# A streaming SSD and gMLP encoder step: GpSimd's weight subtractions become a negated copy on ScalarE and an adding transfer

## The chip, the core and the metric

The kernel runs on one core of one Trainium2 chip. The metric is the device time of one execution in microseconds. Three runs of the kernel before took 1111.30, 1112.45 and 1113.49 us; the median is 1112.45 us. The profile is one execution of its own, with its own time.

Engines are named as in the profile: PE is TensorE (PEld its weight loads), DVE is VectorE, ACT is ScalarE, POOL is GpSimd, SP is SyncE, which only issues transfers here.

## The reference

640 tokens (512 of a prompt, 8 streams of 16 more) go through two layers of width 1024, both with RMSNorm ahead and a residual add behind.

- Layer A is a Mamba-2 mixer: one projection of 1024 to z (2048), x (2048), B (1024), C (1024) and dt (32); a causal convolution of width 4 with SiLU over x, B and C, whose last three input columns are an output too; a chunked state scan of 32 heads in 8 groups; a gate with z and a group norm; a projection back to 1024.
- Layer B is a gMLP: a projection to u, v and z, a LayerNorm of v, a position mix in each of 8 groups, a gate, a projection back.

All of it is float32 with a tight tolerance. The core of layer A, cut:

```
proj = h @ w_in                      # z | x | B | C | dt
xp = concat([conv_prev, xbc]); out = b + sum(w[k] * xp[:, k:k + seq_len])
h_new = h * exp(last) + einsum(B, w_in, x); y = y_in + y_st
return (group_rms_norm(y * silu(z))) @ w_out, xp[:, seq_len:], h_new
```

## The kernel before

**Numbers.** PE multiplies in a reduced float32 format, so each operand is split in two: H is the value rounded to that format, L the rest. A product is three matrix multiplications, H times H, H times L and L times H. For the tokens the tiles are xH and xL, for the weights wh and wl.

**A weight tile** is 128 rows by 1024 columns, 512 KB. `wsplit` (L93 to L104) makes one ready: SP fetches it into `raw` (L95, two buffers), ACT rounds it into `wh` (L99), and then `wl = raw - wh` is made by an engine that the caller names (L100): DVE or POOL. `wh` and `wl` have four buffers each, and a buffer comes free when PE has used the tile.

**The stream of layer A** holds 64 such tiles in the order of their use: for each of the 8 groups x0, x1, B, C, z0, then in the groups 1 to 6 two tiles "o" of the output projection of the group before, then z1; in the first two groups a few stand elsewhere. `Stream.next` hands out a tile and first asks for those that follow, up to `ahead` = 2 (L110 to L135). The set `on_pool` (L316) says whose subtraction POOL makes: the tiles 3 to 6, all z0 and all twelve "o" but the last four tiles of the stream. That is 23 of 63; DVE makes the other 40 (the first tile has its own code).

**A group of layer A.** PE projects x0, x1, B and C tile by tile. Behind each projection `conv_tile` (L406 to L429) does the convolution: DVE moves the result out of PSUM into `xp` with the norm's factor (L411 to L413); POOL clears three columns and copies the cached ones in (L409, L410) and copies the last ones out for the output `nconv` (L415, L416); ACT does the first tap (L418), DVE the other three, each an instruction with two inputs in SBUF (L421); ACT and DVE do the SiLU (L427, L428) into `xc`. PE transposes `xc` to tokens (L468, tile `tp`) for the scan. POOL also makes `xw` (L480), decays old states (L586) and masks some decays `E` (L630). Meanwhile DVE does a chain of five-column steps for the norm (L77 to L86), and ACT the decays `E` of the four heads (L514, L515), which SP reads from `laD` (L512).

**The order.** PE's order is that of the program. In layer A, that of ACT, DVE, POOL and SP is set by a list scheduler when the program is built; each engine then runs its own list strictly in order and waits on semaphores. Layer B (from about 630 us) has its order written out and is touched by none of the changed lines.

Of the kernel before, what the change touches and what calls it, by code (L numbers as in the profile page):

```python
# [8 lines left out]
F32 = mybir.dt.float32  # L9
F32R = mybir.dt.float32r  # L10
I32 = mybir.dt.int32
AF = mybir.ActivationFunctionType
ALU = mybir.AluOpType
# [27 lines left out]
def hybrid_step(ctx: ExitStack, tc: tile.TileContext, xin, xT0, cst, wdt, cache, wA, wAo, h0in, wB, wBv, wBo,  # L41
                lnwb, spc, bsp, nwb, y_out, nconv_out, sspP_out, sspS_out, v_out):
    nc = tc.nc
    V, S, G, T = nc.vector, nc.scalar, nc.gpsimd, nc.tensor
# [17 lines left out]
    def C(n):  # L62
        a, b = _C[n]
        return csb[0][:, a:b] if b <= NCST1 else csb[1][:, a - NCST1:b - NCST1]
# [28 lines left out]
    def wsplit(eng, pool, src, scale=None):  # L93
        raw = (pool or wpool).tile([P, 1024], F32, name="raw", tag="raw", bufs=2)
        nc.sync.dma_start(out=raw, in_=src)  # L95
        H = wpool.tile([P, 1024], F32R, name="wh", tag="wh", bufs=4)
        L = wpool.tile([P, 1024], F32R, name="wl", tag="wl", bufs=4)
        if scale is None:
            S.copy(out=H, in_=raw)  # L99
            eng.tensor_tensor(out=L, in0=raw, in1=H.bitcast(F32), op=ALU.subtract)  # L100
        else:
            S.activation(H, raw, AF.Identity, scale=scale)
            V.scalar_tensor_tensor(L, raw, scale, H.bitcast(F32), ALU.mult, ALU.subtract)
        return H, L  # L104

    class Stream:
# [3 lines left out]
        def fill(self, ahead):  # L110
            while len(self.got) < min(len(self.srcs), self.n + ahead):
                i = len(self.got)
                self.got.append(wsplit(G if i in on_pool else V, self.pools.get(i), *self.srcs[i]))
# [144 lines left out]
    def in_proj(W, xT, pool=None, tag="in", at=(1, 3, 5, 7, 9, 11, 13)):  # L258
        outs = []
        for h, (a, b) in enumerate(HALVES):  # L260
            o = (pool or ps_in).tile([P, 512], F32, name="pin", tag=tag)[:, :b - a]
            outs.append(o)
            for k in range(KD):
                in_proj_step(W, xT, o, h, k)
                if 8 * h + k in at:
                    pump()
        return outs
# [33 lines left out]
    def wo(g):  # L301
        return [(wAo[f],) for f in (2 * g, 2 * g + 1)]

    units, names = [], []
# [8 lines left out]
        names += [p[0] for p in part]  # L313
        units += [p[1:] for p in part]
    units += wo(GROUPS - 2) + wo(GROUPS - 1)
    on_pool = {3, 4, 5, 6} | {i for i, n in enumerate(names) if n in ("z0","o")}  # L316
    stream = Stream(units, 2)


    with ExitStack() as ca:  # L320
# [35 lines left out]
        for d in (15, 13, 11, 9, 7, 5, 3):  # L356
# [17 lines left out]
                        in1=C("blk").rearrange("p (b o) -> p b o", o=1).broadcast_to([P, 8, HEADS]), op=ALU.mult)  # L374
# [31 lines left out]
        def conv_tile(o0, o1, ft, j, cch, nconv):  # L406
            xp = w1.tile([P, 667], F32, name="xp", tag="xp")
            xps = xp[:, 515:667].rearrange("p (b j) -> p b j", j=19)
            G.memset(xp[:, 0:3], 0.0)  # L409
            G.tensor_copy(out=xps[:, :, 0:3], in_=cch[:, j])  # L410
            V.tensor_tensor(out=xp[:, 3:387], in0=o0, in1=rb[:, 0:384], op=ALU.mult)  # L411
            V.tensor_tensor(out=xp[:, 387:515], in0=o1[:, 0:128], in1=rb[:, 384:512], op=ALU.mult)
            V.tensor_tensor(out=xps[:, :, 3:19], in0=o1[:, 128:256].rearrange("p (b j) -> p b j", j=16),  # L413
                            in1=rb[:, 512:640].rearrange("p (b j) -> p b j", j=16), op=ALU.mult)
            G.tensor_copy(out=nconv[:, j, 0, :], in_=xp[:, 512:515])  # L415
            G.tensor_copy(out=nconv[:, j, 1:9, :], in_=xps[:, :, 16:19])  # L416
            acc = w1.tile([P, 667], F32, name="acc", tag="acc")
            S.activation(acc[:, 0:664], xp[:, 0:664], AF.Identity, scale=cw[:, 4 * ft:4 * ft + 1],  # L418
                         bias=cw[:, 128 + ft:129 + ft])
            for k in range(1, 4):  # L420
                V.scalar_tensor_tensor(acc[:, 0:664], xp[:, k:k + 664], cw[:, 4 * ft + k:4 * ft + k + 1], acc[:, 0:664],  # L421
                                       ALU.mult, ALU.add)
            xc = w1.tile([P, NT], F32, name="xc", tag="xc", bufs=5)
            accs = acc[:, 515:667].rearrange("p (b j) -> p b j", j=19)[:, :, 0:16]
            xcs = xc[:, 512:].rearrange("p (b j) -> p b j", j=16)
            for o, a in ((xc[:, :512], acc[:, :512]), (xcs, accs)):
                S.activation(o, a, AF.Tanh)  # L427
                V.scalar_tensor_tensor(o, o, 1.0, a, ALU.add, ALU.mult)  # L428
            return xc  # L429

        cio = conv_io(0)
        pB = in_proj(stream.next(), xT, ps_y, "y")
        xcs = [conv_tile(*o, ft, j, *cio) for j, (o, ft) in enumerate(((px0, 0), (px1, 1), (pB, 16)))]
        side += [cum_sums] + [lambda h=h: by_heads(*h) for h in HALVES]
        pC = in_proj(stream.next(), xT, at=(2, 9, 11))
# [4 lines left out]
        wk = ca.enter_context(tc.tile_pool(name="wk", bufs=2))  # L440

        xcs.append(conv_tile(*pC, 24, 3, *cio))
        pend = {}
        for g in range(GROUPS):
            last = g == GROUPS - 1
            hsl = slice(4 * g, 4 * g + 4)
            if g > 1:
                cio = conv_io(g)
                xcs = [conv_tile(*in_proj(stream.next(), xT), 2 * g, 0, *cio)]
                side.append(pss_)  # L450
                xcs.append(conv_tile(*in_proj(stream.next(), xT, at=(9,)), 2 * g + 1, 1, *cio))
                pump(9)
# [69 lines left out]
            if g:  # L522
                queue(0, *(() if g == 1 else (0,)))
                o = in_proj(stream.next(), xT, ps_m, "m", at=(3, 7, 11, 14))
                xcs.append(conv_tile(*o, 16 + g, 2, *cio))
                queue(1, *(() if g == 1 else (1,)))
                o = in_proj(stream.next(), xT, at=(3, 7, 11, 14))
# [686 lines left out]
```

## Time and profile before

| what | value |
|---|---|
| median of three runs | 1112.45 us (1111.30 to 1113.49) |
| the profiled execution's own time | 1110.38 us |
| its span from the first to the last instruction | 1108.6 us |
| busy share of PE, DVE, ACT, POOL | 94%, 81%, 40%, 18% |
| subtractions of wl on POOL | 23, 55.9 us in all |
| subtractions of wl on DVE in layer A | 40, 50.2 us in all |
| reads from HBM | 106.93 MB |

Busy shares are means over two very different layers. PE is nearly always busy; where it is not, the table of waits names what it waited for. A duration of an engine includes any time that the instruction is held up after its start, so the spread of durations of one kind of instruction is worth as much attention as the mean.

### The profile page before, as it was taken

The page shows a single profiled execution, that of the slowest core. Times are in us where ns is not written, and L with a number is a line of the kernel's source. Part 1 is how long each engine was busy: PE and PEld are TensorE (multiplying, and loading weights), DVE is VectorE, ACT ScalarE, POOL GpSimd, SP SyncE. Part 2 cuts the span into 40 slices and gives each one's busy share as a digit, 9 for nine tenths or more (in the row PEclk, how much of TensorE's full clock was granted, in tenths as well). Part 3 has the DMA queues.
Part 4 walks back from the last instruction along what each step waited for, and adds up shares of the span by engine and source line. Part 5 has one row for each costly group of instructions (what it writes and reads, how often), then busy time and mean ns, then how long its engine had stood idle before and what let it go on. Part 6 is the DMA issues. An engine that isn't in the chain of part 4 may idle for free.

```text
span 1108.6 us, 16897 instructions
## 1 busy us (share of the span) xinstructions
PE 1040.2 (94%) x6387; PEld 936.6 (84%) x6387; DVE 899.4 (81%) x1573; ACT 441.1 (40%) x801; POOL 200.7 (18%) x303
## 2 busy tenths in 40 slices
PE   8998899898998998999999899996899999999996
PEld 7897889798898797888997678886888988988985
DVE  6969897888878878888789866656889889889876
ACT  6363515326254162262552343245333433433343
POOL 2434322404214224042132000000000000000000
PEclk9899999999999999999999999999999999999998
DMA  6463535243362352432622512211423412412322
GB/s 243 146 181 96 170 94 183 85 156 123 91 211 79 89 194 85 156 120 92 211 82 72 171 52 77 69 41 53 124 64 92 124 61 92 122 62 93 89 67 95
DMA packets 56928, 124.88 MB, mean 113 GB/s; under 512 B 9072, under 2 KB 27760, under 8 KB 56848
## 3 DMA queue, kind: packets, MB, share of 16 engines
q1 hardware_dynamic: 56848, 123.82, 35.1%
q8 instruction: 50, 0.82, 0.3%
q14 instruction: 30, 0.25, 0.1%
HBM read 106.93 MB, written 16.86 MB: 112 GB/s over the span
## 4 chain that ended last, share of the span: by engine, by line
PE 53%; DVE 31%; ACT 8%; DMA 4%; issue 3%; SPq 0%; POOL 0%; ACTq 0%; DVEq 0%
PE pop L69 14%; PE pin L69 11%; DVE acc L421 7%; PE pv L69 7%; PE pqb L69 5%; PE pqa L69 4%; PE pqc L69 4%; DMA E<-laD 3%; DVE wf L748 2%; PE st L69 2%; DVE E L630 2%; PE yB L69 1%; DVE xc L428 1%; ACT E L514 1%; DVE rt L85 1%
## 5 line engine op out<-in xcount | busy, mean ns | idle before, releaser
L69 PE MATMUL pin<-xH,wh 128*128 128x384 f32 (+1 forms) x768 | 251.0, 327 | 9.4 <-DVE xp L411 8.6
L69 PE MATMUL pin<-xH,wl 128*128 128x384 f32 (+1 forms) x768 | 240.7, 313 | 0.5 <-DVE wl L100 0.5
L69 PE MATMUL pin<-xL,wh 128*128 128x384 f32 (+1 forms) x768 | 240.5, 313 | 0.0
L69 PEld LDWEIGHTS pin<-xH,wh 128*128 128x128 f32 x768 | 148.4, 193 | 17.7 <-ACT xc L427 9.6
L69 PEld LDWEIGHTS pin<-xL,wh 128*128 128x128 f32 x768 | 148.5, 193 | 0.4 <-issue 0.3
L69 PEld LDWEIGHTS pin<-xH,wl 128*128 128x128 f32 x768 | 147.9, 193 | 0.8 <-DVE wl L100 0.8
L421 DVE SCALAR_TENSOR_TENSOR acc<-xp,cw,acc 128x664 f32<-128x664 f32 x96 | 114.3, 1191 | 17.9 <-ACT acc L418 16.6
L69 PE MATMUL pop<-wf,yHL 128*128 128x512 f32 x480 | 115.3, 397 | 1.1 <-DVE h L964 0.4
L69 PEld LDWEIGHTS pop<-wf,yHL 128*128 128x128 f32 x480 | 89.2, 188 | 25.2 <-DVE h L964 3.1
L748 DVE TENSOR_TENSOR wf<-raw,wf 128x512 fp32r<-128x512 f32 x128 | 86.5, 685 | 29.3 <-ACT wf L747 28.3
L69 PE MATMUL pop<-wh,yHL 128*128 128x512 f32 x320 | 103.4, 404 | 5.8 <-DVE hs L565 5.4
L99 ACT CAST wh<-raw 128x1024 fp32r<-128x1024 f32 x63 | 65.6, 1041 | 103.4 <-PE pin L69 64.7
L747 ACT CAST wf<-raw 128x512 fp32r<-128x512 f32 x128 | 76.4, 617 | 53.9 <-PE pop L69 27.2
L69 PEld LDWEIGHTS pop<-wh,yHL 128*128 128x128 f32 x320 | 57.8, 188 | 21.5 <-DVE hs L565 7.9
L69 PE MATMUL pqa<-xH,wf 128*128 128x320 f32 x256 | 64.3, 320 | 7.3 <-ACT c L1011 7.3
L685 DVE SCALAR_TENSOR_TENSOR h<-pop,rr,h 128x512 f32<-128x512 f32 x80 | 59.0, 743 | 12.7 <-PE pop L69 12.4
L69 PE MATMUL pv<-wh,xL 128*128 128x512 f32 x160 | 62.9, 393 | 2.4 <-DVE xL L231 2.4
L69 PE MATMUL pv<-wh,xH 128*128 128x512 f32 x160 | 63.5, 397 | 0.9 <-DVE xL L231 0.8
L69 PE MATMUL pqb<-tf,wf 128*128 128x320 f32 x384 | 63.0, 313 | 0.9 <-DVE zz L1026 0.9
L69 PE MATMUL pv<-wl,xH 128*128 128x512 f32 x160 | 63.0, 394 | 0.0
L69 PE MATMUL pop<-wl,yHL 128*128 128x512 f32 x160 | 62.6, 391 | 0.0
L514 ACT ACTIVATE E<-E,la 128x128 f32<-128x128 f32 x160 | 51.6, 389 | 17.1 <-DMA E<-laD 12.9
(221 smaller groups left out, 2018.5 us busy)
## 6 DMA issues: line engine op xcount, KB each, us to landing
raw<-wA SPq DMA_DIRECT2D x47, 512.0 KB, 3.8
raw<-wB SPq DMA_DIRECT2D x32, 512.0 KB, 4.0
E<-laD SPq DMA_DIRECT2D x32, 320.0 KB, 6.8
h<-h0in SPq DMA_DIRECT2D x16, 512.0 KB, 4.8
raw<-wAo SPq DMA_DIRECT2D x16, 512.0 KB, 4.1
out_sspS<-h SPq DMA_DIRECT2D x16, 512.0 KB, 3.9
raw<-wBv SPq DMA_DIRECT2D x16, 512.0 KB, 4.2
raw<-wBo SPq DMA_DIRECT2D x16, 512.0 KB, 3.8
```

The lines of the kernel that those rows point to most:

```text
L69: T.matmul(out, lhsT=lhsT, rhs=rhs, start=start, stop=stop, **kw)
L85: V.scalar_tensor_tensor(t, t, -0.5, x, ALU.mult, ALU.mult)
L99: S.copy(out=H, in_=raw)
L421: V.scalar_tensor_tensor(acc[:, 0:664], xp[:, k:k + 664], cw[:, 4 * ft + k:4 * ft + k + 1], acc[:, 0:664], ALU.mult, ALU.add)
L428: V.scalar_tensor_tensor(o, o, 1.0, a, ALU.add, ALU.mult)
L514: S.activation(E_[:, t, :], E_[:, t, :], AF.Relu, bias=la[:, t, h:h + 1], scale=-1.0)
L630: (G if i and (last or e) else V).tensor_tensor(out=Es[2 * i + e], in0=Es[2 * i + e], in1=CBm, op=ALU.mult)
L685: V.scalar_tensor_tensor(h1[:, t, dsl], ps, rg[:, t:t + 1], h1[:, t, dsl], ALU.mult, ALU.add)
L747: S.copy(out=t[:, 0], in_=src)
L748: V.tensor_tensor(out=t[:, 1], in0=src, in1=t[:, 0].bitcast(F32), op=ALU.subtract)
```

## The change

Four edits, all in layer A.

1. For the tiles in `on_pool`, POOL no longer subtracts. ACT writes `-wh` into `wl`, and POOL issues a transfer that reads the weight tile from HBM a second time and adds it to what stands in `wl`.
2. The set `on_pool` loses the tiles 3, 5 and 6, whose subtraction goes to DVE: 20 tiles are left on POOL, 43 are on DVE.
3. The memset of three columns in `conv_tile` goes from POOL to DVE, and its three small copies from POOL to ACT.
4. `ahead` is 3 in place of 2. The buffers stay as many as they were.

```diff
@@ wsplit
             S.copy(out=H, in_=raw)
-            eng.tensor_tensor(out=L, in0=raw, in1=H.bitcast(F32), op=ALU.subtract)
+            if eng is G:
+                S.activation(L, H.bitcast(F32), AF.Identity, scale=-1.0)
+                G.dma_start(out=L, in_=src, accum_op=ALU.add)
+            else:
+                V.tensor_tensor(out=L, in0=raw, in1=H.bitcast(F32), op=ALU.subtract)
@@ the stream
-    on_pool = {3, 4, 5, 6} | {i for i, n in enumerate(names) if n in ("z0","o")}
-    stream = Stream(units, 2)
+    on_pool = {i for i, n in enumerate(names) if n in ("z0","o")}
+    stream = Stream(units, 3)
@@ conv_tile
-            G.memset(xp[:, 0:3], 0.0)
-            G.tensor_copy(out=xps[:, :, 0:3], in_=cch[:, j])
+            V.memset(xp[:, 0:3], 0.0)
+            S.copy(out=xps[:, :, 0:3], in_=cch[:, j])
...
-            G.tensor_copy(out=nconv[:, j, 0, :], in_=xp[:, 512:515])
-            G.tensor_copy(out=nconv[:, j, 1:9, :], in_=xps[:, :, 16:19])
+            S.copy(out=nconv[:, j, 0, :], in_=xp[:, 512:515])
+            S.copy(out=nconv[:, j, 1:9, :], in_=xps[:, :, 16:19])
```

In the lists of the built program, lines behind L100 have numbers that are 4 higher after the change. PE's list is the same in both.

POOL, in the middle of group 3, from the first convolution tile to the token form of x0; `wl<-wA` is z0, the tiles of `wAo` are the two "o". Before:

```order
L415 COPY nconv<-xp 128x3
L416 COPY nconv<-xp 128x24
L100 TENSOR_TENSOR wl<-raw,wh 128x1024
L409 MEMSET xp 128x3
L410 COPY xp<-cch 128x8x3
L415 COPY nconv<-xp 128x3
L416 COPY nconv<-xp 128x24
L100 TENSOR_TENSOR wl<-raw,wh 128x1024
L480 TENSOR_TENSOR xw<-xdt,esu 128x4x128
```

POOL now, the same place and on to the third such tile:

```order
L102 DMA wl<-wA 128x1024
L102 DMA wl<-wAo 128x1024
L484 TENSOR_TENSOR xw<-xdt,esu 128x4x128
L484 TENSOR_TENSOR xw<-xdt,esu 128x128
L102 DMA wl<-wAo 128x1024
```

The subtractions have become transfers at the same places, and the small copies are gone from between them.

ACT in the same group, from the rounding of z0 over the convolutions of x0 and x1. Before:

```order
L514 ACTIVATE E<-E,la 128x128 x4
L99 CAST wh<-raw 128x1024
L418 ACTIVATE acc<-xp,cw 128x664
L515 ACTIVATE E<-E 128x640
L514 ACTIVATE E<-E,la 128x128 x6
L515 ACTIVATE E<-E 128x640
L514 ACTIVATE E<-E,la 128x128
L427 ACTIVATE xc<-acc 128x512
```

ACT now:

```order
L518 ACTIVATE E<-E,la 128x128 x2
L99 CAST wh<-raw 128x1024
L419 COPY nconv<-xp 128x3
L420 COPY nconv<-xp 128x24
L422 ACTIVATE acc<-xp,cw 128x664
L101 ACTIVATE wl<-wh 128x1024
L518 ACTIVATE E<-E,la 128x128 x3
L519 ACTIVATE E<-E 128x640
L518 ACTIVATE E<-E,la 128x128 x2
L431 ACTIVATE xc<-acc 128x512
```

Two copies stand ahead of the first tap (L418, now L422) and the negated copy behind it; between the first tap and the SiLU stand one `L515` and five of the small decay steps where two and seven stood.

SP in the same group, where it reads the four heads' `E` and the weight tiles that follow z0. Before:

```order
L512 DMA E<-laD 128x640
L95 DMA raw<-wAo 128x1024
L512 DMA E<-laD 128x640 x2
L95 DMA raw<-wAo 128x1024
L95 DMA raw<-wA 128x1024
```

SP now:

```order
L95 DMA raw<-wAo 128x1024
L516 DMA E<-laD 128x640 x2
L95 DMA raw<-wAo 128x1024
L516 DMA E<-laD 128x640
L95 DMA raw<-wA 128x1024
```

The last of the four reads of `E` now stands behind the fetch of the second "o".

## Rows read from the trace of the kernel before

**Rows 1.** The page: busy us by engine; a group of instructions, busy us, mean ns.
```profile
PE 1040.2 (94%) x6387; PEld 936.6 (84%) x6387; DVE 899.4 (81%) x1573; ACT 441.1 (40%) x801; POOL 200.7 (18%) x303
...
L421 DVE SCALAR_TENSOR_TENSOR acc<-xp,cw,acc 128x664 f32<-128x664 f32 x96 | 114.3, 1191 | 17.9 <-ACT acc L418 16.6
```

**Rows 2.** Stretches: us, then busy per engine; granted PE clock, DMA share, GB/s.
```profile
234.00:301.00 67.00, 62.88 (x433) 57.57 (x430) 57.24 (x98) 27.76 (x53) 21.11 (x32) 1.00 0.42 131
...
600.00:1108.60 508.60, 477.88 (x2628) 423.97 (x2628) 398.36 (x729) 190.25 (x330) 17.60 (x40) 0.98 0.27 86
```

**Rows 3.** PE's waits in 0 to 600 us: total us, times, longest.
```profile
PE tp L468 <- DVE xc L428: 10.6, 8, 2.9
PE pin L69 <- DVE xp L411: 8.6, 6, 1.9
...
PE st L69 <- DVE h L665: 3.1, 2, 2.9
...
PE yB L69 <- DVE E L630: 1.2, 2, 1.0
```

**Rows 4.** Lines L421 and L100: durations in ns, least/median/most, first and last start.
```profile
L421 DVE SCALAR_TENSOR_TENSOR acc<-xp,cw,acc x96: 894/909/2989, 41.0 to 573.5; 128x664 f32<-128x664 f32 x96
...
L100 DVE TENSOR_TENSOR wl<-raw,wh x40: 1209/1218/2228, 21.4 to 589.7; 128x1024 fp32r<-128x1024 f32 x40
...
L100 POOL TENSOR_TENSOR wl<-raw,wh x23: 2345/2399/2959, 27.3 to 547.5; 128x1024 fp32r<-128x1024 f32 x23
```

**Rows 5.** DVE in time order, group 3: start us, us, line, idle before it.
```profile
253.10 3.25 DVE L421 SCALAR_TENSOR_TENSOR acc<-xp,cw,acc 128x664 f32<-128x664 f32 x2 [1.74 <-ACT acc L418]
...
260.77 2.34 DVE L85 SCALAR_TENSOR_TENSOR rt<-rt,rx 128x5 f32<-128x5 f32 x1
...
270.22 2.24 DVE L421 SCALAR_TENSOR_TENSOR acc<-xp,cw,acc 128x664 f32<-128x664 f32 x1 [1.07 <-ACT acc L418]
...
275.62 0.54 DVE L411 TENSOR_TENSOR xp<-pin,rb 128x384 f32<-128x384 f32 x1
```

**Rows 6.** POOL in time order, group 3: the three subtractions.
```profile
252.30 2.40 POOL L100 TENSOR_TENSOR wl<-raw,wh 128x1024 fp32r<-128x1024 f32 x1 [0.67 <-ACT wh L99]
...
260.69 2.40 POOL L100 TENSOR_TENSOR wl<-raw,wh 128x1024 fp32r<-128x1024 f32 x1 [0.37 <-ACT wh L99]
...
269.38 2.38 POOL L100 TENSOR_TENSOR wl<-raw,wh 128x1024 fp32r<-128x1024 f32 x1
```

**Rows 7.** PE in time order, group 3: the two waits, first use of an "o".
```profile
268.70 0.63 PE L468 MATMUL tp<-csb,xc 128*128 128x128 f32 x4 [1.33 <-DVE xc L428]
...
276.31 0.41 PE L69 MATMUL pin<-xH,wh 128*128 128x384 f32 x1 [1.90 <-DVE xp L411]
...
285.33 0.39 PE L69 MATMUL pop<-wl,yHL 128*128 128x512 f32 x1
```

**Rows 8.** Stretches as in Rows 2: a wait, and stretches at half clock.
```profile
347.20:349.20 2.00, 0.07 (x2) 0.04 (x1) 1.97 (x4) 0.79 (x3) 1.06 (x4) 1.00 0.15 61
349.68:353.09 3.41, 3.41 (x14) 3.31 (x13) 3.37 (x8) 1.98 (x3) 1.32 (x2) 0.50 0.06 16
...
103.92:107.33 3.41, 3.41 (x26) 3.19 (x27) 2.27 (x4) 2.39 (x3) 2.13 (x3) 0.50 0.90 302
```

**Rows 9.** ACT: all roundings; a small instruction; a stretch as in Rows 2.
```profile
L99 ACT CAST wh<-raw 128x1024 fp32r<-128x1024 f32 x63 | 65.6, 1041 | 103.4 <-PE pin L69 64.7 <-PE pop L69 32.4 <-DMA raw<-wA 6.3
...
L340 ACT ACTIVATE nea<-csb x1: 231/231/231, 21.6 to 21.6; 128x32 f32<-128x32 f32 x1
...
257.00:264.00 7.00, 7.00 (x50) 6.93 (x49) 6.69 (x19) 6.85 (x16) 3.04 (x5) 1.00 0.11 44
```

**Rows 10.** Transfers: KB, median us to landing; one issue on SP.
```profile
E<-laD SPq DMA_DIRECT2D x32, 320.0 KB, 6.8
...
raw<-wAo SPq DMA_DIRECT2D x16, 512.0 KB, 4.1
...
254.72 0.33 SPq L95 DMA_DIRECT2D raw<-wAo  x1
```

## The prediction

> **What bounds the kernel now.** I read the page first, then the stretches, PE's waits, and one group of layer A in order of time. PE is busy 94% of the span [rows 1], so no other engine's time counts by itself: only what PE waits for, and what its clock loses. Layer B is 508.6 us in which POOL works 17.6 [rows 2]; none of the edits is there. In layer A a group takes some 73 us, and in a stretch of 67 us PE works 62.9, DVE 57.2, ACT 27.8 and POOL 21.1 [rows 2]. PE's waits there [rows 3] are nearly all for DVE: 10.6 us for the convolved tile (`tp` for `xc`) and 8.6 us for a PSUM bank that DVE empties (`pin` for `xp`), 14 waits and 19.2 us in all.
>
> Why is DVE late? The convolution step L421 has a median of 909 ns, but a mean of 1191 and up to 2989 [rows 1, 4]: 96 x 0.282 = 27 us above the median. In group 3 the long ones stand where POOL subtracts. POOL subtracts from 252.30 to 254.70, 260.69 to 263.09 and 269.38 to 271.76 [rows 6]. DVE's two steps at 253.10 take 3.25 us where two medians are 1.82; a five-column step at 260.77 takes 2.34 us and ends 0.02 us after the subtraction; the step at 270.22 takes 2.24 [rows 5]. That is 1.4 + 2.2 + 1.3 = 4.9 us in one group. Right behind, PE waits 1.33 us at 268.70 and 1.90 us at 276.31, the second until L411, which starts at 275.62 [rows 5, 7]. So the two waits of a group, 3.2 us, are smaller than what the subtractions cost DVE on the way to them.
>
> **The change part by part.**
>
> *Subtraction off POOL.* 20 of the 23 subtractions go. What holds DVE up 4.9 us a group goes with them, if a transfer's issue on POOL does not hold DVE in the same way (a rival below). The waits of 19.2 us lie in groups 1 to 7. Of these I take 17, not all: DVE's own work stays, and its other neighbours on POOL (xw, the mask) stay too. Bounds: 0 to 19.2. In group 0 the waits of PE for masked decays and old states, 1.2 and 3.1 us [rows 3], also stand behind a held DVE; I take 3 of 4.3.
>
> *The clock.* After a long wait PE's granted clock falls from 2.4 to 1.2 GHz: it waited until about 349.2, and from 349.68 it ran 3.41 us at 0.50 [rows 8]. There are five such stretches between 100 and 435 us, the first at 103.92; each follows one of the waits above of 1.9 us or more. At half the clock 3.41 us do the work of 1.7, so five cost 8.5 us. Waits of about 1.9 us did not always bring one (the one before 276.31 did not: clock 1.00 from 234 to 301 [rows 2]). I take 6 of 8.5 back; bounds 0 and 8.5, and a shifted program may catch a fall elsewhere, 1.7 each.
>
> *Three subtractions to DVE* (the tiles 3, 5, 6, before 65 us): 3 x 1.22 = 3.7 us of DVE [rows 4], in place of three on POOL of 2.40 each that held DVE up for 1.3 to 2.2 us [rows 5, 6], 4 to 6.6 in all. I take 0; bounds -3 to +4.
>
> *The negated copy:* 20 on ACT. The rounding of the same tile takes 1.04 us [rows 9]; no row shows the copy, so 20 x 1.04 = 21 us of ACT, bounded by 0.23 (a 32-column instruction) and 1.04 each. It stands behind the first tap, and ahead of the SiLU that ACT used to wait for. ACT is 40% busy [rows 1], but in 257 to 264 it works 6.85 of 7 us [rows 9]. What covers the copy is that fewer decay steps stand ahead of the SiLU now, and idle time behind 264. Without that cover it costs 1.04 us twice a group.
>
> *Small copies:* three on ACT per convolution tile, 96 in all. For 32 columns a row shows 0.23 us [rows 9]; two of them stand ahead of the first tap, on the path from `xp` to DVE: 0.46 us x 4 tiles = 1.8 us a group. The memset on DVE is no longer than 0.23: 0.9 a group. Against DVE's 4.9 that leaves 2.2 to 3, about the 3.2 of PE's waits; this is why I keep 17 and not 19.2. Since the first copy can run while DVE still fills the rest of `xp`, the real price should be nearer to half.
>
> *The adding transfer.* Bytes as a fetch of `raw`, which lands after 4.1 us [rows 10]; it also reads and writes SBUF. Ends: 4.1 us, and twice the slowest kind of row, 2 x 6.8 = 13.6. I take 6, near the row with the same bytes. The tightest tile is the second "o" of a group: its subtraction began at 269.38 [rows 6]; now the first tap and the negated copy come before its issue, about 271; PE needs it at 285.33 [rows 7], 3.2 earlier if the waits go. That leaves 11 us. z0 and the first "o" have 19 and more. At 6 us nothing waits; at 13.6 us PE would wait 2.6 us in six groups, 16 us. POOL's own time for an issue lies between 0.33 (SP's [rows 10]) and 2.40, what it replaces; behind it on POOL stands `xw`, as before.
>
> *Fetch order and `ahead`.* The fourth read of `E` stands behind the fetch of the second "o", which waits for a `raw` buffer. That fetch went out at 254.72 [rows 10], when the subtraction of z0 ended (254.70); now the rounding frees the buffer, 2.4 us sooner. `E` lands 6.8 us later, ahead of its use; 0, at most 1 us a group. Four buffers for `wh` and `wl` bound the lookahead, not `ahead`: 0.
>
> **Sum.** 17 + 3 + 6 = 26 us off the profiled execution's 1110.4 us (span 1108.6): 1084.4. The median is 2.1 above that execution, so 1086.5 us.
>
> **Rivals.**
>
> *ACT takes DVE's place.* For it: ACT is full from 257 to 264, and copies stand on the path. Against: it idles much of the rest. If all 1.8 us of copies and two negated copies (2.1) come onto the path, 1 of DVE's 4.9 us is left, a third of the waits go at most, and the clock still falls: 6 + 3 = 9 us, 1103.
>
> *The issue on POOL holds DVE as the subtraction did.* For it: it is the same engine, and an issue may take up to 2.40 us. Against: an issue reads no tile. Then only the small copies moved, for nothing: 1110 to 1114, so 1112.
>
> *The adding transfer comes late.* One mechanism: PE reaches the second "o" before `wl` has landed. It decides from 11 us after the issue; beyond that each microsecond counts six times. At 20 us it costs 9 x 6 = 54 against 26 won: 1140; from about 15.3 us on the kernel is slower than before. Against: a plain fetch of the same bytes takes 4.1.
> The Trainium skill, "Collectives: The Full Stack", section "The bandwidth ceiling: the fold count and why AG ≠ RS ≠ AR", says that a transfer that adds needs two source reads per piece and so runs at half the rate of a copy. By that, as an estimate, it would land after some 8 us: within the 11, so the sum stays; no row here shows such a transfer. The skill's "SBUF — State Buffer", "Who interferes with whom", adds that GpSimd cannot write descriptors while DVE runs a copy or tensor_scalar in its two-port mode. A row shows a DVE step and a POOL subtraction finishing together [rows 5, 6]; whether descriptors wait likewise, none shows. It would add at most such a step's length, and I leave the rival's chance as it is.
>
> **How the numbers follow.** Forecast 0.62 (own range 1076 to 1097), ACT in DVE's place 0.20 (1097 to 1109), POOL's issue holds DVE 0.07, late transfer 0.11. All waits and falls of the clock together, 19.2 + 4.3 + 8.5 + 3 = 35 us, give 1077 as the best; the range goes from 1076 to 1107, which leaves the late transfer and most of the hold outside. A difference under 0.2%, 2.2 us, is what a measurement cannot tell from none. Faster by more: 0.62 + 0.20 and 0.01 of the hold, 0.83; the same 0.05; slower 0.01 + 0.11 = 0.12.
>
> **What would show it.** Right: L421's most falls under 1.7 us and its mean to about 1.0; PE's two waits of a group (for `xc`, for `xp`) shrink under 0.5 us; half-clock stretches between 100 and 435 us go from five to one or two; layer B takes 508 us as before. Wrong: PE waits named for a transfer into `wl`; the first tap L418 waiting on ACT's own list, so that ACT's idle time before the SiLU is gone while PE's waits stay; DVE steps as long as POOL's issues beside them.

## The result and the profile after

The changed kernel takes 1083.99 us (median of 4 runs, 1083.10 to 1087.49), the kernel before 1112.64 beside it: ratio 0.9756, 95% interval 0.9732 to 0.9780. The profiled execution took 1084.73 us at a span of 1083.0.

All of it is in layer A. Layer B begins at the first `pv`, at 626.3 us before and at 600.1 after, 26.2 us sooner. The page and the stretches, as in [rows 1, 2]: the page's line of engines, then the whole of layer A before, and then, of after, layer A and a piece of group 3.

```profile
PE 1032.2 (95%) x6387; PEld 932.8 (86%) x6387; DVE 862.7 (80%) x1608; ACT 470.2 (43%) x917; POOL 127.0 (12%) x172
```
```profile
0.00:626.30 626.30, 586.86 (x3875) 531.45 (x3875) 525.66 (x900) 257.23 (x481) 183.09 (x263) 0.98 0.43 137
```
```profile
0.00:600.10 600.10, 578.90 (x3876) 527.79 (x3876) 488.43 (x935) 286.24 (x597) 107.26 (x132) 0.98 0.55 160
225.00:292.00 67.00, 66.05 (x458) 60.66 (x458) 55.84 (x106) 32.03 (x69) 12.12 (x16) 1.00 0.56 157
```

PE's idle time in layer A went from 626.3 - 586.9 = 39.4 us to 600.1 - 578.9 = 21.2, so 18.2 us less. Its busy time fell by 8.0, for the same matmuls. DVE lost 37 us, although it got three subtractions more. Layer B, from its first `pv` to the end, takes 1108.6 - 626.3 = 482.3 us before and 1083.0 - 600.1 = 482.9 after, with PE busy for 453.3 us in both. The stretch of 508.6 us in [rows 2] begins at 600 us, where layer A still has 26.3 us to run, so it isn't the length of layer B that the prediction takes it for.

The lines that answer to [rows 4]; the taps' row also as a group, with its mean, as in [rows 1]:

```profile
L425 DVE SCALAR_TENSOR_TENSOR acc<-xp,cw,acc x96: 894/910/1632, 37.9 to 547.1; 128x664 f32<-128x664 f32 x96
...
L104 DVE TENSOR_TENSOR wl<-raw,wh x43: 1212/1226/2227, 21.3 to 563.4; 128x1024 fp32r<-128x1024 f32 x43
...
L102 POOL DMA_DIRECT2D wl<-wAo x12: 861/876/907, 108.2 to 470.4; - x12
```
```profile
L425 DVE SCALAR_TENSOR_TENSOR acc<-xp,cw,acc 128x664 f32<-128x664 f32 x96 | 94.7, 987 | 30.7 <-ACT acc L422 29.5
```

The taps' most fell from 2989 to 1632 ns and their mean from 1191 to 987; the median is as it was. I use one measure for this below: the taps' excess, 96 times mean minus median. Before it is 96 x 0.282 = 27.1 us, after 96 x 0.077 = 7.4. It is only a part of what is held (the five-column steps of [rows 5] are held too), but two rows give it for every kernel.

The whole of it can be counted from the trace: for every DVE step, the time above the median of its own line and shape, where that is more than 60 ns. Before, there are 66 such steps with 67.0 us above their medians in all, and every one of them stands beside a POOL instruction; 37.6 us stand beside the subtractions, 12.0 beside the masks, 10.6 beside `xw`. After, 50 steps with 27.9 us are left, every one again beside a POOL instruction, and none of it falls to the issue of a transfer. (A step beside two POOL instructions counts for the one that it overlaps longer.) I call this sum the held time.

One group of after in time order, to set against [rows 5, 6]: POOL, then DVE.

```profile
246.43 0.90 POOL L102 DMA_DIRECT2D wl<-wA  x1 [33.72 <-ACT wl L101]
253.79 0.87 POOL L102 DMA_DIRECT2D wl<-wAo  x1 [6.46 <-ACT wl L101]
```
```profile
245.09 2.80 DVE L425 SCALAR_TENSOR_TENSOR acc<-xp,cw,acc 128x664 f32<-128x664 f32 x3 [1.36 <-ACT acc L422]
...
251.63 0.17 DVE L85 SCALAR_TENSOR_TENSOR rt<-rt,rx 128x5 f32<-128x5 f32 x1
252.47 0.91 DVE L425 SCALAR_TENSOR_TENSOR acc<-xp,cw,acc 128x664 f32<-128x664 f32 x1 [0.47 <-ACT acc L422]
...
253.90 2.56 DVE L425 SCALAR_TENSOR_TENSOR acc<-xp,cw,acc 128x664 f32<-128x664 f32 x2
```

Three taps take 2.80 us across the issue at 246.43, against three medians of 2.73. The step that took 2.34 takes 0.17. What is still long is the pair at 253.90, beside POOL's `xw` (254.35 to 255.74).

PE's waits in 0 to 600 us, as in [rows 3] (total, times, longest), and the stretches that run at half clock between 100 and 435, as in [rows 8]:

```profile
PE pop L69 <- DVE hs L569: 4.7, 5, 1.0
PE tp L472 <- DVE y L655: 4.4, 1, 4.4
PE pin L69 <- DVE xp L413: 1.9, 1, 1.9
```
```profile
108.26:111.67 3.41, 3.40 (x12) 3.41 (x13) 3.41 (x6) 2.17 (x6) 0.80 (x2) 0.50 0.85 324
125.33:128.74 3.41, 3.41 (x14) 3.32 (x13) 2.53 (x7) 3.12 (x7) 0.00 (x0) 0.50 0.67 134
```

The two waits of every group, `tp` for `xc` and `pin` for `xp` (19.2 us), are gone. In group 1 stand two new ones, of 4.4 and 1.9 us, and the two half-clock stretches that are left follow them.

### The profile page after: what moved, and what is told of

It reads as the page before. It is cut to its first block, busy times and chain, and to the rows that moved or that the text cites. A ratio compares the mean times of both kernels' runs of the same rounds, so it can differ in the third digit from the quotient of the medians.

```text
span 1083.0 us, 16928 instructions
## 1 busy us (share of the span) xinstructions
PE 1032.2 (95%) x6387; PEld 932.8 (86%) x6387; DVE 862.7 (80%) x1608; ACT 470.2 (43%) x917; POOL 127.0 (12%) x172
## 4 chain that ended last, share of the span: by engine, by line
PE 62%; DVE 20%; ACT 5%; issue 3%; DMA 2%; SPq 0%; ACTq 0%; DVEq 0%
PE pin L69 26%; PE pop L69 11%; PE pv L69 9%; DVE wf L752 3%; PE pqb L69 3%; PE pqa L69 2%; PE pqc L69 2%; PE st L69 2%; DVE h L968 2%; PE yB L69 2%; DVE uu L1063 1%; PE tp L472 1%; DVE thb L1062 1%; DVE uu L1066 1%; ACT wf L751 1%
## 5 line engine op out<-in xcount | busy, mean ns | idle before, releaser
L425 DVE SCALAR_TENSOR_TENSOR acc<-xp,cw,acc 128x664 f32<-128x664 f32 x96 | 94.7, 987 | 30.7 <-ACT acc L422 29.5
L104 DVE TENSOR_TENSOR wl<-raw,wh 128x1024 fp32r<-128x1024 f32 x43 | 53.6, 1245 | 9.2 <-ACT wh L99 9.1
```

Source lines behind the costliest of these rows:

```text
L104: V.tensor_tensor(out=L, in0=raw, in1=H.bitcast(F32), op=ALU.subtract)
```

## The experiments

Three theories. **Theory 1:** a POOL instruction that reads SBUF holds DVE's two-input instructions; held, DVE is late for PE, and PE's clock falls behind the waits. **Theory 2:** the gain comes from the small copies or from the deeper fetch. **Theory 3:** POOL's own results (`xw`, masks) were late behind its subtractions, and DVE's lengthened steps were hidden. Each ratio is to the kernel before, run beside it.

### The change taken apart

The first two parts alone; the copies stay on POOL and the fetch two ahead.
```
-    stream = Stream(units, 3)
+    stream = Stream(units, 2)
...
-            V.memset(xp[:, 0:3], 0.0)
-            S.copy(out=xps[:, :, 0:3], in_=cch[:, j])
+            G.memset(xp[:, 0:3], 0.0)
+            G.tensor_copy(out=xps[:, :, 0:3], in_=cch[:, j])
...
```


> The kernel before with the first two parts of the change alone: the negated copy on ScalarE, the adding transfer for z0 and o, the three subtractions of the first tiles on VectorE. The small convolution copies stay on GpSimd, and the fetch stays two tiles ahead. Theory 1 (GpSimd's subtraction stretches VectorE's two-input instructions beside it, VectorE is then late for TensorE): 1084 to 1092 us, ratio to before 0.974 to 0.982, the second tap near 1.0 us in the mean, PE's waits at tp<-xc and pin<-xp gone from the groups. Theory 2 (the gain comes from the small copies or the deeper fetch): 1105 us or more.

Measured: 1084.98 us, 0.9775 (0.9742 to 0.9808). Taps' mean 1004 ns; the two waits are gone, though one of 6.4 us stands in group 1. So these first two parts bring all but what these runs can tell apart.

Only the small copies and the memset moved off GpSimd:
```
-            G.tensor_copy(out=xps[:, :, 0:3], in_=cch[:, j])
+            S.copy(out=xps[:, :, 0:3], in_=cch[:, j])
...
```


> The kernel before with the small convolution copies and the memset moved off GpSimd, and nothing else; all 23 subtractions stay on GpSimd. Theory 1: 1108 to 1116 us, the taps stay near 1.19 us in the mean. Theory 2 (the copies were what conv waited for): 1095 us or less.

Measured: 1105.66 us, 0.9955 (0.9937 to 0.9973), 5 us better, which neither theory expected. The taps' mean is 1155 ns; in the profiled execution, the longest of the ten with 1109.19 us, `tp` for `xc` and `pin` for `xp` still cost 9.8 and 10.4 us, and the held time is 66.6 us, much as before. So Theory 1 doesn't explain the gain, and why it is there is open. On top of the first two parts, these copies and the deeper fetch together were worth 0.1% by the medians and 0.2% by the ratios, within both intervals.

Only the fetch, three tiles ahead:
```
-    stream = Stream(units, 2)
+    stream = Stream(units, 3)
```


> The kernel before with the fetch three tiles ahead in place of two, and nothing else. Theory 1: 1112 us within 3 either way, since no wait of TensorE before the change ends on a weight tile's transfer in layer A. Theory 2 (the order of the subtractions is what counts): 1100 us or less.

Measured: 1110.98 us, 1.000 (0.9982 to 1.0018). Theory 2 falls on this part. But this kernel too has a wait of PE for `y`, 3.9 us, in group 1.

Every subtraction on VectorE, with no adding transfer at all:
```
-    on_pool = {i for i, n in enumerate(names) if n in ("z0","o")}
+    on_pool = set()
```


> The changed kernel with every subtraction on VectorE, so neither a subtraction on GpSimd nor an adding transfer; fetch and copies as changed. It adds 20 subtractions of 1.2 us, 24 us, to VectorE, 2.4 to 3.6 a group. Theory 1: VectorE pays 1.2 us a tile where the subtraction on GpSimd cost it 37.6/20 = 1.9 us of stretched instructions, so this lands between the two kernels: 1088 to 1106 us. Theory 3 (what counted was GpSimd's own lateness with xw and the states, VectorE's time is hidden): 1082 to 1087 us. If VectorE's slack is used up, no gain is left: 1108 us or more, and then the transfer and not the mere removal is what the change needs.

Measured: 1087.08 us, 0.9790 (0.9759 to 0.9822): a microsecond under Theory 1's range, and at the upper end of Theory 3's. The rows say how; the group of the taps and that of the subtractions:

```profile
L425 DVE SCALAR_TENSOR_TENSOR acc<-xp,cw,acc 128x664 f32<-128x664 f32 x96 | 93.6, 975 | 5.8 <-ACT acc L422 4.5
L104 DVE TENSOR_TENSOR wl<-raw,wh 128x1024 fp32r<-128x1024 f32 x63 | 78.2, 1241 | 11.4 <-ACT wh L99 11.4
```

DVE's idle time ahead of the taps falls from 30.7 to 5.8 us: 20 subtractions, 78.2 - 53.6 = 25 us, went into idle time. So what matters is that the subtraction leaves POOL; where it goes is worth 0.3% by the ratios, with intervals that overlap. By itself this fits Theory 3 as well. The trace of the kernel before speaks against Theory 3. These are all its waits for an instruction of POOL by another engine:

```profile
ACT hl L492 <- POOL xw L480: 1.7, 1, 1.7
ACT acc L418 <- POOL nconv L415: 1.7, 6, 0.3
```

Neither PE nor DVE waits for POOL there, nor in any other run here. The next four runs show what load on POOL does by itself.

### Load put back on GpSimd

An idle subtraction behind each adding transfer, the same tile on both sides:
```
+                G.tensor_tensor(out=idle[0], in0=H.bitcast(F32), in1=H.bitcast(F32), op=ALU.subtract)
...
```


> The changed kernel, and behind each of the 20 adding transfers GpSimd runs an idle subtraction of 128x1024 (the high half minus itself, into a tile that nothing reads), so GpSimd is loaded as before but nobody waits for what it computes. It leaves nothing out and adds idle work. Theory 1 (the subtraction holds VectorE): VectorE's instructions beside it are stretched again, the second tap's mean goes from 0.99 back towards 1.19 us, PE's waits per group come back: 1100 to 1112 us. Theory 3 (only the lateness of GpSimd's own results counted): xw and the masks on GpSimd are late again, taps stay near 0.99: 1095 us or more with no stretched taps. If neither: 1084 to 1088.

The same with the operands of before:
```
+                G.tensor_tensor(out=idle[0], in0=raw, in1=H.bitcast(F32), op=ALU.subtract)
...
```


> The changed kernel, and behind each of the 20 adding transfers GpSimd runs the subtraction of before (raw minus high half, two tiles of 128x1024) into a tile that nothing reads. Adds idle work, leaves nothing out. The idle subtraction with one tile on both sides took 1.89 us, held VectorE for 20.1 us and gave 1096. Theory 1 (the hold is set by the form of GpSimd's instruction): this one takes near 2.4 us, holds VectorE for 32 to 40 us, the taps' mean is 1.15 to 1.2 us, and the time is 1102 to 1110 us. Rival (the hold is the smaller part, and the late low half was the rest of the loss): 1094 to 1099 us again, with taps below 1.1 us.

Measured: 1096.09 us, 0.9880 (0.9857 to 0.9903), and 1103.66 us, 0.9934 (0.9916 to 0.9952). The first lies 4 us below Theory 1's range, for it had less hold: its subtraction takes 1.92 us, that with two tiles 2.42. Of the second kernel POOL, then DVE, then the taps' group, then PE's waits:

```profile
247.82 2.40 POOL L105 TENSOR_TENSOR idle<-raw,wh 128x1024 f32<-128x1024 f32 x1 [31.80 <-ACT wh L101]
...
256.39 2.40 POOL L105 TENSOR_TENSOR idle<-raw,wh 128x1024 f32<-128x1024 f32 x1 [5.34 <-DVE rr L86]
```
```profile
248.78 4.04 DVE L429 SCALAR_TENSOR_TENSOR acc<-xp,cw,acc 128x664 f32<-128x664 f32 x3 [1.35 <-ACT acc L426]
...
256.50 2.32 DVE L85 SCALAR_TENSOR_TENSOR rt<-rt,rx 128x5 f32<-128x5 f32 x1
```
```profile
L429 DVE SCALAR_TENSOR_TENSOR acc<-xp,cw,acc 128x664 f32<-128x664 f32 x96 | 109.2, 1137 | 26.5 <-ACT acc L426 25.3
```
```profile
PE tp L476 <- DVE xc L436: 8.0, 10, 1.5
PE pin L69 <- DVE xp L419: 7.1, 6, 1.3
```

Nobody reads what these subtractions compute, and yet the five-column step is back at 2.32 us, ending with POOL's (258.79 and 258.82), and PE's two waits are back with 15 of the 19.2 us. The loss follows the dose. The taps' excess is 7.4 us after, 96 x (1081 - 910) = 16.4 with one tile, 96 x (1137 - 910) = 21.8 with two, 27.1 before. Ratios times 1111 us put the three 13.8, 19.8 and 27.1 us above after: 1.5, 1.4 and 1.4 us per microsecond of excess. By the held time, 27.9 us after, 47.2 with one tile, 58.6 with two and 67.0 before, it is 0.7, 0.6 and 0.7. A late POOL remains as a small part at most: the `xw` and masks here wait behind the idle work too, but PE and DVE never wait for POOL, and what PE waits for again is `xc` and `xp`, as Theory 1 says.

An idle copy, one input:
```
+                G.tensor_copy(out=idle[0], in_=H.bitcast(F32))
...
```


> The changed kernel, and behind each adding transfer GpSimd copies the high half (128x1024, one input) into the idle tile. Adds idle work, leaves nothing out. Theory 1 with two inputs needed for the hold: 1083 to 1089 us; with one input enough: 1090 to 1105 us. Theory 3: between the changed kernel and the one with the idle subtraction by GpSimd's busy time alone.

Measured: 1084.44 us, 0.9771 (0.9740 to 0.9802). By the time alone, two inputs would be needed for a hold. The rows say otherwise: POOL's copy, and DVE beside it.

```profile
251.25 1.03 POOL L105 COPY idle<-wh 128x1024 f32<-128x1024 f32 x1 [4.94 <-ACT wh L101]
```
```profile
251.34 0.96 DVE L85 SCALAR_TENSOR_TENSOR rt<-rt,rx 128x5 f32<-128x5 f32 x1
...
252.41 0.90 DVE L429 SCALAR_TENSOR_TENSOR acc<-xp,cw,acc 128x664 f32<-128x664 f32 x1
```

The step of 0.17 us takes 0.96 and ends with the copy, at 252.30 and 252.28. But the next tap begins at 252.41, in the changed kernel at 252.47: the hold fell into time in which DVE waited for ACT. The same step takes 0.96 to 1.05 us beside the copy in four groups, and 4.6 us are held beside the copies in all. So one input holds as well; here, where the hold is short and in part lands in slack, it cost nothing that the time shows.

Three idle memsets, which read nothing:
```
+                for _ in range(3):
+                    G.memset(idle[0], 0.0)
...
```


> The changed kernel, and behind each adding transfer GpSimd sets the idle tile (128x1024) three times to zero: GpSimd is busy about as long as with a subtraction, but reads nothing. Adds idle work, leaves nothing out. Theory 1: no instruction of VectorE is stretched, 1083 to 1089 us. Theory 3: GpSimd's own results are as late as beside a subtraction, so the same time as with the idle subtraction (1095 us or more).

Measured: 1087.03 us, 0.9800 (0.9771 to 0.9829). It isn't the control it was meant to be. The memsets depend on nothing, so POOL ran all 60 from 0.8 to 90.0 us instead of beside the groups. What it does show is the stretch 0 to 58 us, and the taps in it:

```profile
0.00:58.00 58.00, 49.53 (x275) 45.80 (x276) 42.79 (x89) 29.99 (x55) 49.44 (x53) 0.89 0.58 188
```
```profile
L430 DVE SCALAR_TENSOR_TENSOR acc<-xp,cw,acc x7: 895/895/910, 42.1 to 56.5; 128x664 f32<-128x664 f32 x7
```

POOL is busy 49.4 of 58 us, and none of the seven taps is lengthened. For two-input steps, the Trainium skill states this in "SBUF — State Buffer", section "Who interferes with whom": a DVE instruction with two SBUF inputs contends with a GpSimd instruction that reads SBUF, and not with one that only writes it. Taps, copy and memsets agree, with the 0.96 us beside the copy and the 895 ns beside the memsets. A step of another kind was lengthened beside a memset, though:

```profile
32.83 1.08 DVE L214 TENSOR_SCALAR dg<-csb,rs 128x128 f32<-128x128 f32 x1 [1.76 <-PE pb L69]
```

In the changed kernel all five of these steps take 0.28 or 0.29 us. This one ends at 33.91, just behind a memset from 32.88 to 33.83. So the memsets show that two-input taps aren't held by writes, not that writes hold nothing.

### What else stands on GpSimd

The mask products moved to VectorE, in the changed kernel:
```
-                    (G if i and (last or e) else V).tensor_tensor(out=Es[2 * i + e], in0=Es[2 * i + e], in1=CBm, op=ALU.mult)
+                    V.tensor_tensor(out=Es[2 * i + e], in0=Es[2 * i + e], in1=CBm, op=ALU.mult)
```


> The changed kernel with the mask products of a group (five per group were GpSimd's) all on VectorE. In the changed kernel the masks on GpSimd still stretch VectorE by 11.4 us in all and PE waits 0.95 us a group behind them. Theory 1: 1076 to 1083 us, ratio to the changed kernel 0.993 to 0.999. Theory 3 (GpSimd's share of the work was worth having): 1085 us or more.

Measured: 1075.01 us, 0.9686 (0.9661 to 0.9712), the fastest of all: another 0.7% from the change, with intervals that don't meet. (Nine products were GpSimd's in all, not five a group as the expectation has it.) The masks' group in the changed kernel, on DVE and on POOL, then in this one, and two of its stretches:

```profile
L634 DVE TENSOR_TENSOR E<-E,CBm 128x640 f32<-128x640 f32 x23 | 28.8, 1263 | 0.1
...
L634 POOL TENSOR_TENSOR E<-E,CBm 128x640 f32<-128x640 f32 x9 | 17.1, 1905 | 2.9 <-DVE CBm L605 1.5 <-issue 1.4
```
```profile
L634 DVE TENSOR_TENSOR E<-E,CBm 128x640 f32<-128x640 f32 x32 | 26.1, 824 | 0.1
```
```profile
150.00:300.00 150.00, 149.89 (x1036) 137.57 (x1035) 123.26 (x233) 70.92 (x145) 20.82 (x30) 1.00 0.57 163
300.00:450.00 150.00, 150.00 (x1036) 138.84 (x1035) 123.17 (x235) 76.98 (x165) 21.66 (x31) 1.00 0.60 175
```

DVE does all 32 products in less time than 23 of them beside POOL's nine, 26.1 us against 28.8. PE's waits for `hs`, 4.7 us in the changed kernel, are gone. PE then is busy 299.9 of 300 us: there is nothing left in the middle groups but PE's own work.

The same in the kernel before, without the change (the diff is the same):

> The kernel before with its mask products on VectorE alone, and nothing of the change. Theory 1 (holds add up, each instruction of GpSimd with its own): what the masks were worth in the changed kernel, 6 to 12 us, so 1098 to 1106 us, the subtraction's stretching unchanged at about 38 us. Rival (GpSimd was overloaded, and any part taken off it frees the rest): 1095 us or less. Rival (VectorE has no room for them while it is stretched): 1110 us or more.

Measured: 1102.16 us, 0.9919 (0.9897 to 0.9941). That is 9 us; in the changed kernel 0.7% are 8. The subtraction's hold stays (taps' mean 1192 ns; 39.6 us held beside the subtractions, 37.6 before), so the holds add up, as far as the intervals tell, each with its own price.

`xw` on VectorE as well:
```
-                    G.tensor_tensor(out=xw[:, ta:tb, r_], in0=xdt[:, ta:tb, r_], in1=ev, op=ALU.mult)
+                    V.tensor_tensor(out=xw[:, ta:tb, r_], in0=xdt[:, ta:tb, r_], in1=ev, op=ALU.mult)
...
```


> The changed kernel with GpSimd's mask products and its 32 xw products on VectorE too. With the masks alone moved it was 1075; xw on GpSimd still stretches VectorE by 8.7 us there. By the hold alone: VectorE gets 32 products worth about 12 us by the xdt product's own time, and loses 8.7 us of stretching, so 1072 to 1078 us, the same within what can be told. If xw's place in VectorE's order holds up the taps: 1079 us or more.

Measured: 1080.16 us, 0.9721 (0.9702 to 0.9741), no better than the masks alone and probably worse. The taps are now clean, and PE has one new wait:

```profile
L425 DVE SCALAR_TENSOR_TENSOR acc<-xp,cw,acc 128x664 f32<-128x664 f32 x96 | 87.1, 907 | 20.2 <-ACT acc L422 19.5
```
```profile
PE pin L69 <- ACT xc L431: 7.7, 1, 7.7
```

The excess is gone and the kernel is 4 us (by the ratios) to 5 us (by the medians) slower than with the masks alone, with intervals that overlap a little. It isn't that `xw` holds up the taps, as the expectation had it: DVE's idle time ahead of them is 20.2 us, 30.8 with the masks alone. Nor does the wait of 7.7 us, in group 1, account for it, since two waits of 4.2 and 1.8 us stand there with the masks alone. In the profiled executions most of the distance is there before: PE begins `pla`, in group 0, at 47.1 us, with the masks alone at 43.3, after a mean granted clock up to there of 0.89 against 1.00; behind the waits of group 1 it is 3.3 us, at layer B 5.5. Whether that belongs to the kernel or to these two executions was not tried.

The adding transfer for 13 tiles more, with the masks on VectorE:
```
-    on_pool = {i for i, n in enumerate(names) if n in ("z0","o")}
+    on_pool = {i for i, n in enumerate(names) if n in ("z0","o","z1","C") and i > 7}
...
```


> The changed kernel with the masks on VectorE, and the adding transfer for the C and z1 tiles too (from the eighth tile on), so about 14 more subtractions of 1.22 us leave VectorE, and ScalarE gets as many copies of 1.04 us. If VectorE's time were still what TensorE waits for: 1065 to 1073 us. If VectorE has slack for its subtractions (all 20 moved back to it cost 3 us at most): 1074 to 1078 us. If the transfers crowd the loads of the decay tiles: 1080 us or more.

Measured: 1092.10 us, 0.9823 (0.9806 to 0.9840), 15 us (by the ratios) to 17 us (by the medians) slower than with the masks alone, although DVE is freer. The chain that ended last in 190 to 270 us: with the masks alone its shares by line, then, of this kernel, pieces in order of time (start us, us, what):

```profile
by line: PE pin L69 65.8%; PE pop L69 18.3%; PE st L69 4.3%; PE yB L69 3.2%; PE tp L472 3.0%; PE yA L69 2.2%; PE cb L69 1.6%; PE yq L69 1.2%; PE pss L69 0.5%; issue 0.1%
```
```profile
235.52 6.50 DMA out_sspS<-h
242.54 6.06 DMA E<-laD
248.63 1.57 ACT E L518 x5
...
253.69 0.85 ACT acc L422
254.57 0.91 DVE acc L425
```

With the masks alone PE makes its own chain. Here the chain of a group goes through a store of states, the load of `E`, ACT's decay steps and ACT's first tap to DVE. `E`'s median time to landing is 7.0 us, 5.6 with the masks alone. So both the transfers and ACT (33 negated copies in place of 20) are now late; the run doesn't part them. Not all of the loss can be theirs: `i > 7` also gives the subtraction of group 0's z0 back to DVE (14 tiles more, one less), and in the profiled executions `pla` begins at 47.5 us in place of 43.3, behind a wait for DVE of 3.8 us, ahead of the first adding transfer. That is 4.2 us of the 14.1 by which layer B begins later.

## Why the prediction was right

Forecast 1086.5 us (1084.4 for the profiled execution), measured 1083.99 (1084.73). Step by step:

- **The mechanism** was right. POOL's subtraction holds DVE, and DVE's lateness is what PE waits for: taking the load away removes it, putting idle load back brings it back in proportion.
- **PE's waits**, 17 + 3 = 20 us taken: PE's idle time in layer A fell by 18.2 in all. All 19.2 us of the groups' waits went, more than the 17; group 0's left 0.8 and 0.9 us in place of 3.1 and 1.2; the new waits in group 1 took 6.3 back.
- **The clock**, 6 us taken: half-clock stretches between 100 and 435 us went from five to two, as forecast, worth 3 x 1.7 = 5.1. PE's busy time fell by 8.0; the other 2.9 I can't assign.
- **The sum**, 26 us, against 25.6 of the span: that it fits so closely is luck in part. Idle time came out 1.8 us under its term and busy time 2.0 above the clock's, and the 6.3 us of new waits in group 1 were in no term.
- **Three subtractions to DVE**, 0: not separated. All 20 others moved there too cost 0.3% by the ratios, so the term is small.
- **Negated copy**, 1.04 us on ACT and covered: 1.046 x 20, and ACT's lateness did show (DVE's idle time ahead of the taps rose from 17.9 to 30.7 us) but no group wait of PE came from it. With 13 more of them it did, or the transfers did: the rival "ACT takes DVE's place" names a real limit that lies beyond this dose.
- **Small copies** were mis-sized. They take 0.20, 0.19 and 0.21 us and the memset 0.06, near the 0.23 taken; but I priced them as a cost against the gain, and alone they gain 5 us, for a reason that stays open.
- **The adding transfer**, 6 us: it lands after 5.3 to 9.8 us, median 5.7, and PE waits for no `wl` that it makes. These rows give the medians by source, beside plain fetches of the same size:

```profile
raw<-wA SPq DMA_DIRECT2D x47, 512.0 KB, 3.8
...
raw<-wAo SPq DMA_DIRECT2D x16, 512.0 KB, 4.8
...
wl<-wAo POOLq DMA_DIRECT2D x12, 512.0 KB, 5.5
wl<-wA POOLq DMA_DIRECT2D x8, 512.0 KB, 6.9
```

The Trainium skill's "Collectives: The Full Stack", section "The bandwidth ceiling: the fold count and why AG ≠ RS ≠ AR", gives a ReduceScatter in a ring half the rate of an AllGather, because its add reads two sources; the prediction carried this over to a transfer within one core. That is not what the "o" tiles show (5.5 to 4.8) and close to what the z0 tiles show (6.9 to 3.8). Here it changed nothing.
- **The issue on POOL** takes 0.86 to 1.01 us and holds no DVE step beside it in the group shown (the three taps take 2.80 us); in the whole trace no held time falls to an issue. That rival fell.
- **Fetch order**, 0 and at most 1 us a group: the fetch alone measures 1.000. But the bound failed in group 1, where PE's new wait of 4.4 us stands on the chain behind a load of `E`:

```profile
99.19 5.03 DMA E<-laD
...
104.93 0.93 ACT wh L99
...
106.08 0.85 ACT acc L422
...
106.95 0.91 DVE acc L425
107.86 0.27 DVE y L655
```

`E` lands at 104.2; ACT then does a decay step, a rounding, the copies and its first tap before DVE reaches `y`, which PE waits for. A wait of 3.9 us for `y` is there with the deeper fetch alone, and one of 6.4 for `xp` without it. So group 1 is tight in each of these; what would free it was not settled.

## What to carry to other kernels

When one line's most is three times its median, look at which other engine works in just those instances. If it is GpSimd reading SBUF beside VectorE's two-input steps, count the held time against VectorE's own price for the work: here VectorE did it for less than being held cost. Then stop at the point where the transfers and ScalarE still have slack; the same edit on 13 more tiles, with VectorE freer, made the kernel 15 to 17 us slower, of which some 4 were lost ahead of its first adding transfer.

## What the runs showed of the hardware

- A GpSimd copy of 1.03 us held a five-column VectorE step from 0.17 to 0.96 us: one SBUF input on GpSimd is enough. Memsets beside seven two-input taps held none (895 to 910 ns), but a `tensor_scalar` of 128x128 beside a memset took 1.08 us in place of 0.29.
- All 66 VectorE steps that ran over 60 ns above the median of their kind in the kernel before stood beside a GpSimd instruction.
- GpSimd's subtraction with one tile on both sides took 1.92 us, with two tiles 2.42.
- GpSimd's issue of an adding transfer of 512 KB took 0.88 us in the median, and the transfer landed after 5.7.
